# Five row buffers instead of four for the expert gathers of a one-core encoder block

## The chip, the cores and the metric

The kernel runs on one core of a Trainium2 chip. The metric is the device time of one execution in microseconds; the median of the runs shown counts.

## The reference, cut to what matters

One layer of a streaming encoder on 1024 tokens of width 1024: eight heads of stick-breaking attention and four mLSTM heads share an input projection, their outputs go through an output projection, and a PEER mixer follows. For this change only the mixer matters. Each token picks 128 of 16384 experts (8 heads, 16 each); expert e is one row of `expert_u` and one row of `expert_v`, 1024 floats each:

```
u   = take(expert_u, idx)            # 128 rows per token
act = gelu(einsum('td,tkd->tk', x, u))
vv  = take(expert_v, idx)
y   = einsum('tk,tkd->td', gate * act, vv)
```

## The kernel before, in words

The first part (to about 1400 us in the trace) is attention, mLSTM, output projection and routing. After that the mixer is computed for the 1024 tokens in two different ways that run beside one another.

**Gathered tokens.** The first 384 tokens (three tiles of 128, `NH` = 3) are done by `gather` (line 897). For each tile and each of its 128 choices k, GpSimd (POOL) issues an indirect DMA that fetches one row of U for each of the 128 tokens into a row buffer `gu` of 128x1024 floats (line 918), and VectorE (DVE) multiplies it with the tokens and sums along the row (line 920). When all 128 are done, ScalarE makes the gelu. Then the same with V: an indirect DMA into a row buffer `gv` (line 929), and DVE adds the row times its gate to `gy` (line 931). `gu` and `gv` have one tag and so share one set of `GU` buffers, used in turn. Two times 128 gathers for three tiles are 768, each of 128 rows of 4 KB. At a tile's end the buffers also take `x1` and `g2` (lines 933 to 942), and the result is written.

**Dense tokens.** The other 640 tokens are done by `dense` (line 1032): for each of 128 blocks of 128 experts, the block of U is loaded (`uf`, line 1015), split into two parts for TensorE (`uh`, `ul`, line 121 on ScalarE and line 125 on DVE), and multiplied with the tokens (`da`, lines 129 to 131); 24 of the blocks (`AHEAD`) were multiplied earlier and their gelu outputs `dg` are read back from memory (line 1012). `dg` is multiplied with the gates `dw` on DVE (line 1051) and split into `dgh` and `dgl`. The block of V is loaded into a single buffer `vf` (line 1042), split into `vh` and `vl`, and the second product runs in groups of three blocks: a part stays in PSUM (`yr`), another is copied out by ScalarE (`dt`, line 1092) and added on DVE (`dy`, line 1093). After the last block, line 1065 adds `x1` for eight row groups (`dx`) and line 1067 writes them.

**What sets the order.** `build` weaves the two generators (line 1208). A scheduler then fixes, when the program is built, the order of the instructions on each engine by its own estimate of how long each takes; on the chip each engine runs its own list in that order and waits on semaphores. So a DVE instruction that waits for a gather holds up the dense instructions behind it on DVE. The weights and blocks of U and V are issued from SyncE (SP), the gathers from POOL.

```
for k in range(ns):
    vv = g.tile([P, D], F32, tag="gu", name=f"gv{T}_{k}", bufs=GU)
    nc.gpsimd.indirect_dma_start(out=vv, out_offset=None, in_=a["V"],
                                 in_offset=bass.IndirectOffsetOnAxis(ap=idx[:, k : k + 1], axis=0))
    nc.vector.scalar_tensor_tensor(out=y, in0=vv, scalar=A[:, k : k + 1], in1=y, op0=ALU.mult, op1=ALU.add)
    yield G_STEP
```

Of the kernel before, what the change touches and what calls it, by code (L numbers as in the profile page):

```python
# [49 lines left out]
NB = 128  # L50

GB = 3
GU = 4
DG = 3
N_A = (8, 16)

# [56 lines left out]
class Kernel:  # L113
# [783 lines left out]
    def gather(self, T):  # L897
# [18 lines left out]
        for k in range(ns):  # L916
            u = g.tile([P, D], F32, tag="gu", name=f"gu{T}_{k}", bufs=GU)
            nc.gpsimd.indirect_dma_start(out=u, out_offset=None, in_=a["U"],  # L918
# [8 lines left out]
# [6 lines that stand above are left out]
        x1 = g.tile([P, D], F32, tag="gu", name=f"gx1_{T}", bufs=GU)  # L933
        if half:
            nc.sync.dma_start(x1[0:n], y[n:P])
            nc.vector.tensor_add(y[0:n], y[0:n], x1[0:n])
            x1 = g.tile([P, D], F32, tag="gu", name=f"gx2_{T}", bufs=GU)
        nc.sync.dma_start(x1[0:n], self.x1t_d[0:n, T])
        g2 = g.tile([P, D], F32, tag="gu", name=f"g2_{T}", bufs=GU)
        nc.sync.dma_start(g2[0:n], self.g2_d.partition_broadcast(n))  # L940
# [336 lines left out]
```

## Time and profile before

| | |
|---|---|
| Time, median of 3 runs | 3395.37 us (3392.22 to 3406.84) |
| The profiled execution | 3403.98 us, span 3402.3 us |
| Busy share of the span | PE 91%, DVE 79%, ACT 49%, POOL 44% |
| Mean granted TensorE clock | 0.957 |
| Moved | 799.51 MB, mean 235 GB/s |

The profiled execution is one run, 8.6 us above the median; sums over the trace are made against its own 3403.98 us. PE is TensorE, PEld its weight loads, DVE VectorE, ACT ScalarE, POOL GpSimd, SP SyncE. A wait is put down to the work whose end came last before the waiting engine went on.

### The profile page before, as it was taken

How to read it: one execution, taken by the hardware profiler on the slowest of the kernel's cores; microseconds unless marked ns; L12 is line 12 of the kernel's file. 1: busy time of each engine (PE TensorE's matmuls, PEld its weight loads, DVE VectorE, ACT ScalarE, POOL GpSimd, SP SyncE). 2: the span in 40 equal slices, each digit the busy share in tenths (PEclk: the TensorE clock that was granted, in tenths of full speed). 3: DMA queues.
4: the chain of work that ended last, by engine and by line, in shares of the span. 5: the costliest groups of instructions: out<-in, count | busy, mean ns of one | idle time of the engine just before them, and what ended most of it. 6: DMA issues, size and time to landing. Idle time of an engine off the chain costs nothing.

```text
span 3402.3 us, 53484 instructions
## 1 busy us (share of the span) xinstructions
PE 3085.2 (91%) x18581; PEld 2802.9 (82%) x18581; DVE 2698.6 (79%) x5464; ACT 1673.5 (49%) x3646; POOL 1493.9 (44%) x1334
## 2 busy tenths in 40 slices
PE   6998998998888789999899999999999999999993
PEld 4666676666666789999899999999999999999993
DVE  6776764589989858886778888888888887888887
ACT  4765677855675887885233333333333333333321
POOL 3000004545767334233455455565555545555554
PEclk8999998899989899999999999999999999999997
DMA  5243325532333545699888999998989998999988
GB/s 183 77 132 130 115 78 179 162 94 82 104 114 101 175 155 180 219 340 317 283 279 309 312 312 304 318 332 299 330 301 319 313 314 291 334 325 315 306 290 276
DMA packets 388864, 799.51 MB, mean 235 GB/s; under 512 B 35033, under 2 KB 216793, under 8 KB 386033
## 3 DMA queue, kind: packets, MB, share of 16 engines
q1 hardware_dynamic: 268368, 387.03, 34.7%
q0 software_dynamic: 110624, 402.77, 33.9%
q10 hardware_dynamic: 9600, 6.29, 0.6%
q8 instruction: 146, 2.39, 0.3%
q14 instruction: 126, 1.02, 0.1%
HBM read 716.23 MB, written 79.73 MB: 234 GB/s over the span
## 4 chain that ended last, share of the span: by engine, by line
PE 24%; DMA 21%; DVE 20%; issue 18%; POOL 10%; ACT 5%; SPq 1%; POOLq 0%; DVEq 0%; ACTq 0%
DMA gv<-in_V_dram,idx 11%; POOL gu L918 7%; DMA gu<-in_U_dram,idx 3%; DMA vf<-in_V_dram 3%; DVE gy L931 3%; POOL gv L929 2%; DVE gu L920 2%; PE wps L998 1%; PE da L129 1%; PE da L131 1%; PE da L130 1%; PE z L494 1%; ACT wm L994 1%; PE ipc L129 1%; PE ipc L131 1%
## 5 line engine op out<-in xcount | busy, mean ns | idle before, releaser
L918 POOL DMA_INDIRECT gu<-in_U_dram,idx x384 | 505.7, 1317 | 527.3 <-DVE gu L920 471.1
L929 POOL DMA_INDIRECT gv<-in_V_dram,idx x384 | 501.7, 1307 | 442.6 <-DVE gy L931 372.5
L931 DVE SCALAR_TENSOR_TENSOR gy<-gv,gA,gy 128x1024 f32<-128x1024 f32 x384 | 492.0, 1281 | 93.4 <-DMA gv<-in_V_dram,idx 88.8
L920 DVE SCALAR_TENSOR_TENSOR gu<-gu,gh 128x1024 f32<-128x1024 f32 x384 | 466.0, 1223 | 122.4 <-DMA gu<-in_U_dram,idx 116.9
L1092 ACT COPY dt<-dy 128x384 f32<-128x384 f32 x336 | 158.9, 480 | 455.0 <-PE dy L131 313.7
L129 PE MATMUL dy<-dgh,vh 128*128 128x384 f32 x1024 | 348.9, 344 | 34.6 <-ACT dt L1092 34.4
L129 PE MATMUL da<-dah,uh 128*128 128x384 f32 x1024 | 349.1, 341 | 10.9 <-ACT dg L946 6.4
L130 PE MATMUL dy<-dgl,vh 128*128 128x384 f32 x1024 | 348.6, 341 | 0.0
L131 PE MATMUL da<-dah,ul 128*128 128x384 f32 x1024 | 346.8, 339 | 0.5 <-DVE ul L125 0.5
L131 PE MATMUL dy<-dgh,vl 128*128 128x384 f32 x1024 | 347.3, 340 | 0.0
L130 PE MATMUL da<-dal,uh 128*128 128x384 f32 x1024 | 346.8, 339 | 0.0
L129 PE MATMUL yr<-dgh,vh 128*128 128x256 f32 x1024 | 286.6, 288 | 33.4 <-ACT dgh L121 21.2
L130 PE MATMUL yr<-dgl,vh 128*128 128x256 f32 x1024 | 292.0, 288 | 11.4 <-DVE dgl L125 11.2
L131 PE MATMUL da<-h2h,ul 128*128 128x256 f32 x1024 | 290.8, 284 | 0.0
L129 PE MATMUL da<-h2h,uh 128*128 128x256 f32 x1024 | 290.7, 284 | 0.0
L130 PE MATMUL da<-h2l,uh 128*128 128x256 f32 x1024 | 290.5, 284 | 0.0
L131 PE MATMUL yr<-dgh,vl 128*128 128x256 f32 x1024 | 287.3, 286 | 0.7 <-DVE vl L125 0.4
L121 ACT CAST vh<-vf 128x1024 fp32r<-128x1024 f32 x128 | 134.2, 1049 | 285.4 <-DMA vf<-in_V_dram 280.2
L125 DVE TENSOR_TENSOR vl<-vf,vh 128x1024 fp32r<-128x1024 f32 x128 | 156.4, 1222 | 93.1 <-ACT vh L121 92.8
L129 PEld LDWEIGHTS dy<-dgh,vh 128*128 128x128 f32 x1024 | 196.2, 192 | 40.1 <-ACT dt L1092 39.6
L125 POOL TENSOR_TENSOR vlm<-kvrm,vhm 128x128 fp32r<-128x128 f32 x56 | 30.3, 542 | 452.1 <-ACT vhm L121 442.9
L129 PEld LDWEIGHTS yr<-dgh,vh 128*128 128x128 f32 x1024 | 196.3, 195 | 37.4 <-ACT dgh L121 23.7
(435 smaller groups left out, 8941.0 us busy)
## 6 DMA issues: line engine op xcount, KB each, us to landing
uf<-in_UT_dram SPq DMA_DIRECT2D x128, 512.0 KB
vf<-in_V_dram SPq DMA_DIRECT2D x128, 512.0 KB
w_d<-wst SPq DMA_DIRECT2D x19, 2048.0 KB
dw<-w_d SPq DMA_DIRECT2D x32, 1216.0 KB
wfwq<-in_w_q_dram SPq DMA_DIRECT2D x192, 128.0 KB
wada<-in_w_adaT_dram SPq DMA_DIRECT2D x64, 256.0 KB
wfwo<-in_w_out_dram SPq DMA_DIRECT2D x96, 128.0 KB
wada<-in_w_adaT_dram SPq DMA_DIRECT2D x16, 512.0 KB
```

The costliest lines, as they stand in the source:

```text
L121: nc.scalar.copy(hi, src)
L125: e.tensor_sub(lo, src, hi.bitcast(F32))
L129: mm(out, sh, mh, start=start, stop=False, skip_group_check=skip)
L130: mm(out, sh, ml, start=False, stop=False, skip_group_check=skip)
L131: mm(out, sl, mh, start=False, stop=stop, skip_group_check=skip)
L494: mm(z[e], k[kx][r], q[qx][r, ts], start=i == 0, stop=i == 2 * len(k) - 2)
L918: nc.gpsimd.indirect_dma_start(out=u, out_offset=None, in_=a["U"], in_offset=bass.IndirectOffsetOnAxis(ap=idx[:, k : k + 1], axis=0))
L920: nc.vector.scalar_tensor_tensor(out=u, in0=u, scalar=1.0, in1=h2, op0=ALU.mult, op1=ALU.mult, accum_out=A[:, k : k + 1])
L929: nc.gpsimd.indirect_dma_start(out=vv, out_offset=None, in_=a["V"], in_offset=bass.IndirectOffsetOnAxis(ap=idx[:, k : k + 1], axis=0))
L931: nc.vector.scalar_tensor_tensor(out=y, in0=vv, scalar=A[:, k : k + 1], in1=y, op0=ALU.mult, op1=ALU.add)
L994: nc.scalar.activation(m[:, t], o1[:, :, t], AF.Copy, scale=i2g[:, 1, col])
L1092: nc.scalar.copy(t, ps)
```

## The change

```
-GU = 4
+GU = 5
```

The number of row buffers that `gu`, `gv`, and the `x1` and `g2` tiles share goes from four to five. Each takes 4 KB in every partition; the pool `gp` grows by that much into memory that nothing else holds at the time. No instruction is added or taken away. POOL waits, before it issues a gather, for the DVE instruction that read the buffer's last content: with four buffers that is the gather four back, with five the one five back. The scheduler, which plans with this, puts the gathers' instructions in other places among the dense ones.

On POOL, at the first gathers (`gu_0` is the first; what a row waits for is in brackets), before:

```order
L918 DMA gu_3_17980<-in_U_dram,idx 128x1024
L918 DMA gu_4_17983<-in_U_dram,idx 128x1024 [waits DVE_49]
L918 DMA gu_5_17986<-in_U_dram,idx 128x1024 [waits DVE_49]
```

and with the change:

```order
L918 DMA gu_3_17980<-in_U_dram,idx 128x1024
L918 DMA gu_4_17983<-in_U_dram,idx 128x1024
L918 DMA gu_5_17986<-in_U_dram,idx 128x1024 [waits DVE_49]
```

The fifth gather no longer waits for DVE; the order on POOL is the same but for one `dw` load that comes four gathers later.

On DVE, around the last block's multiply by the gates (line 1051, block 127; `gv_k` is choice k of the last tile), before:

```order
L125 TENSOR_TENSOR vl_35193<-vf_35190,vh_35192 128x1024
L1093 TENSOR_TENSOR dy<-dy,dt_35101 128x384
L931 SCALAR_TENSOR_TENSOR gy_32439<-gv_103_34767,gA_29433,gy_32439 128x1024
L1051 TENSOR_TENSOR dg_35131<-dg_35131,dw_34753 128x640
L931 SCALAR_TENSOR_TENSOR gy_32439<-gv_104_34840,gA_29433,gy_32439 128x1024
L125 TENSOR_TENSOR dgl_35198<-dg_35131,dgh_35197 128x640
```

and with the change:

```order
L125 TENSOR_TENSOR vl_35193<-vf_35190,vh_35192 128x1024
L1093 TENSOR_TENSOR dy<-dy,dt_35101 128x384
L931 SCALAR_TENSOR_TENSOR gy_32439<-gv_113_35113,gA_29433,gy_32439 128x1024
L1051 TENSOR_TENSOR dg_35131<-dg_35131,dw_34753 128x640
L931 SCALAR_TENSOR_TENSOR gy_32439<-gv_114_35116,gA_29433,gy_32439 128x1024
L125 TENSOR_TENSOR dgl_35198<-dg_35131,dgh_35197 128x640
```

The dense instructions stand alike; ten gathers that stood behind this place now stand ahead of it. Of the 768 gather instructions on DVE, 55 stood ahead of block 0's line 1051 and 59 do now, 389 and 397 ahead of block 64's, 744 and 754 ahead of block 127's.

On DVE, behind the last addition of line 1093, before:

```order
L1093 TENSOR_TENSOR dy<-dy,dt_35335 128x384
L1065 SCALAR_TENSOR_TENSOR dx_3_35371<-yr_17823,mod,dx_3_35371 128x256
L1065 SCALAR_TENSOR_TENSOR dx_3_35371<-dy,mod,dx_3_35371 128x384
L931 SCALAR_TENSOR_TENSOR gy_32439<-gv_111_35107,gA_29433,gy_32439 128x1024
L1065 SCALAR_TENSOR_TENSOR dx_4_35376<-yr_17824,mod,dx_4_35376 128x256
```

and with the change:

```order
L1093 TENSOR_TENSOR dy<-dy,dt_35335 128x384
L1065 SCALAR_TENSOR_TENSOR dx_3_35371<-yr_17823,mod,dx_3_35371 128x256
L1065 SCALAR_TENSOR_TENSOR dx_3_35371<-dy,mod,dx_3_35371 128x384
L931 SCALAR_TENSOR_TENSOR gy_32439<-gv_121_35207,gA_29433,gy_32439 128x1024
L1065 SCALAR_TENSOR_TENSOR dx_4_35376<-yr_17824,mod,dx_4_35376 128x256
```

Seventeen gathers (111 to 127) followed the last addition, now seven (121 to 127) do; the last of them stands ahead of `dx_6`, where it stood behind `dx_7`.

## Rows read from the trace of the kernel before

**Rows 1.** Windows by stage: window, length, busy time of each engine, clock, DMA share, GB/s.
```profile
1411.00:1600.00 189.00, 184.52 (x1317) 182.25 (x1316) 143.52 (x250) 149.35 (x402) 62.88 (x57) 0.99 0.91 325
1600.00:1800.00 200.00, 171.37 (x1098) 168.04 (x1097) 140.53 (x214) 58.80 (x95) 87.44 (x66) 0.94 0.83 282
1800.00:3340.00 1540.00, 1478.92 (x9863) 1467.00 (x9863) 1308.15 (x1634) 488.93 (x805) 834.30 (x627) 0.99 0.91 312
3340.00:3403.00 63.00, 9.86 (x60) 8.89 (x58) 42.12 (x49) 3.84 (x8) 23.49 (x20) 0.62 0.79 271
```
**Rows 2.** The page's chain that ended last, shares of the span by line.
```profile
DMA gv<-in_V_dram,idx 11%; POOL gu L918 7%; DMA gu<-in_U_dram,idx 3%; DMA vf<-in_V_dram 3%; DVE gy L931 3%; POOL gv L929 2%; DVE gu L920 2%; PE wps L998 1%; PE da L129 1%; PE da L131 1%; PE da L130 1%; PE z L494 1%; ACT wm L994 1%; PE ipc L129 1%; PE ipc L131 1%
```
**Rows 3.** The page's costliest groups: busy, mean ns, idle before and its releaser.
```profile
L918 POOL DMA_INDIRECT gu<-in_U_dram,idx x384 | 505.7, 1317 | 527.3 <-DVE gu L920 471.1
L929 POOL DMA_INDIRECT gv<-in_V_dram,idx x384 | 501.7, 1307 | 442.6 <-DVE gy L931 372.5
L931 DVE SCALAR_TENSOR_TENSOR gy<-gv,gA,gy 128x1024 f32<-128x1024 f32 x384 | 492.0, 1281 | 93.4 <-DMA gv<-in_V_dram,idx 88.8
```
**Rows 4.** The gather instructions by tile: durations (min/median/max), first and last start.
```profile
L918 POOL DMA_INDIRECT gu<-in_U_dram,idx x384: 935/1281/1987, 1411.2 to 3077.2; - x192
L929 POOL DMA_INDIRECT gv<-in_V_dram,idx x384: 935/1277/3151, 1816.2 to 3387.9; - x192
```
**Rows 5.** Waits of DVE, 1600 to 3340 us: total, times, longest.
```profile
DVE gu L920 <- DMA gu<-in_U_dram,idx: 97.6, 93, 3.4
DVE vl L125 <- ACT vh L121: 87.0, 35, 9.1
DVE gy L931 <- DMA gv<-in_V_dram,idx: 78.7, 85, 3.7
```
**Rows 6.** Waits of PE, 1600 to 3340 us.
```profile
PE dy L129 <- ACT dt L1092: 33.6, 17, 7.1
PE yr L129 <- ACT dgh L121: 21.2, 12, 3.6
PE yr L129 <- ACT vh L121: 12.3, 4, 4.3
PE yr L130 <- DVE dgl L125: 11.2, 9, 2.7
```
**Rows 7.** Waits of ACT, 1600 to 3340 us.
```profile
ACT vh L121 <- DMA vf<-in_V_dram: 280.2, 76, 11.2
...
ACT dt L1092 <- DVE dy L1093: 119.7, 46, 4.9
```
**Rows 8.** Timeline of DVE at the end: start, duration, instruction, idle before.
```profile
3336.88 0.82 DVE L1051 TENSOR_TENSOR dg<-dg,dw 128x640 f32<-128x640 f32 x1
...
3352.97 0.55 DVE L1093 TENSOR_TENSOR dy<-dy,dt 128x384 f32<-128x384 f32 x1
3358.71 0.48 DVE L1065 SCALAR_TENSOR_TENSOR dx<-yr,mod,dx 128x256 f32<-128x256 f32 x1 [5.19 <-DMA dx<-x_d]
...
3376.01 0.61 DVE L1065 SCALAR_TENSOR_TENSOR dx<-dy,mod,dx 128x384 f32<-128x384 f32 x1
...
3397.37 1.23 DVE L942 TENSOR_TENSOR gy<-gy,gx 128x1024 f32<-128x1024 f32 x1
```
**Rows 9.** The chain near the end: two gathers' way, issue to landing.
```profile
3375.97 6.45 DMA gv<-in_V_dram,idx
...
3387.95 6.75 DMA gv<-in_V_dram,idx
```
**Rows 10.** DMA queues, 1600 to 3400 us: packets, MB, share of 16 engines.
```profile
q0 software_dynamic: 102672, 373.86, 59.5%
q1 hardware_dynamic: 119037, 178.30, 30.2%
```
**Rows 11.** Timeline of POOL at the first gathers.
```profile
1415.32 0.94 POOL L918 DMA_INDIRECT gu<-in_U_dram,idx  x1 [0.30 <-issue]
1427.39 0.94 POOL L918 DMA_INDIRECT gu<-in_U_dram,idx  x1 [11.14 <-DVE gu L920]
```

## The prediction

> **What bounds the kernel now.** I read first the windows by stage, then the chain, then who waits for whom, and last the timeline of the end. The change touches nothing before the first gather at 1411.2 us [rows 4], so only what follows counts. There the windows [rows 1] show two things that are nearly full at once. PE is busy for 1650 of the 1740 us between 1600 and 3340 us (171.37 and 1478.92 added), so 90 us are idle. The DMA engines are at 0.83 and 0.91 at 282 and 312 GB/s. DVE is busy for 1449 us. From 3340 us on PE has 9.86 us of work left, and the end belongs to the gathers.
>
> The chain [rows 2] tells which of the two ends last. The gathers' way (DMA `gv` 11% and `gu` 3%, POOL's issues 7% and 2%, DVE's uses 3% and 2%) is 28% of the span, some 950 us; the `vf` loads are 3%, some 102 us. The gathers run in a circle: POOL waits for DVE to free a buffer (471.1 and 372.5 us) [rows 3], the rows fly, DVE uses them. One gather follows another every 2.58 us (1976.7 us from first start to last, over 767 steps) [rows 4], so a round of four buffers takes 10.3 us.
>
> The circle costs the dense work through DVE's list. DVE stands 176.3 us for gathers in flight (97.6 and 78.7) and 87.0 us for `vh` [rows 5], and what is behind it stands too. PE's own waits [rows 6] are 78.3 us in four rows.
>
> **The change, part by part.** No instruction is added. A gather may be issued when the DVE use five back is over, not the one four back, so up to one step, 2.58 us, earlier. The scheduler also moves the gathers forward in DVE's list: by 4 at the first dense block, by 10 at the last one.
>
> *The start.* The first four gathers leave by 1415.32 us and the fifth waits 11.14 us for DVE [rows 11]; it can now leave about 10.7 us earlier, 0.30 us behind the fourth's end. Nothing at the end hangs on this alone. I count it with the ten gathers below.
>
> *The dense stretch.* The 178 waits for gathers are 0.99 us each on average, the longest 3.7 us [rows 5]. If a gather left 2.58 us sooner and flew as long, nearly all would vanish; if it flew longer for having one more beside it, some would stay. I take half. What that is worth is read from PE. The waits for `dgh` (21.2) and `dgl` (11.2) come from DVE's list. `dt` (33.6 us) comes late either because DVE's additions are (119.7 us) or because ACT stands in front of a `vf` load (280.2 us) [rows 7]; I put half of it, 16.8 us, down to DVE. That makes 49 us, of which the gathers cause 176.3 in 263.3 (the rest is `vh`), so 33 us, and half of this is **16 us** off. The bounds are nothing, if PE then waits for `vf` instead, and the full 49 us.
>
> *The ten gathers more.* They must now be done before the dense work ends. Their DVE time, 10 times 1.281 us [rows 3], falls into a DVE that is idle for 15% of 1800 to 3340 us. Their bytes, 10 times 0.524 MB, would take 16.8 us at 312 GB/s if the DMA engines had no room, and nothing if they had; at a share of 0.91 [rows 1] the engines have 9% of 1540 us, some 139 us, to spare. So between 0 and 17 us on; I take **5 us**, nearer to the free end.
>
> *The end.* From the end of the last `dy` addition (3352.97 plus 0.55) to the end of the span (3402.3) it is 48.8 us [rows 8]. Seventeen gathers stand there now; with the change seven, of which five fit in buffers at once. With the `dx` steps as late as before, the use of 121 is over 7.4 us and that of 122 10.2 us behind that addition (one gather step behind each `dx` row, as before: 5.2 us of waiting, 1.1 of `dx`, 1.28 of use); the last gather is issued then and lands 6.75 us later [rows 9], so the last use ends near 18.5 us. But `dx_7` then decides: before, it was done at 3376.62, 23.1 us behind the addition; the final addition (1.23 us) stands behind it now, and its write takes as long as before, 3.7 us (3402.3 less 3398.60), so 28 us; the write of `dx_7` itself, at a flight of about 6.5 us, ends near 30. From 48.8 to 30 makes **19 us** off. Bounds: 10 us if `dx` itself gets later, 24 if it gets earlier with less traffic. This term rests on the two lists, not on a bandwidth, and I trust it most.
>
> The sum against the profiled execution: 3404.0 - 16 + 5 - 19 = 3374 us. That execution stands 8.6 us above the median of the runs, so against the median it is **3365 us**.
>
> **A rule weighed.** A gather takes 6.45 and 6.75 us from issue to landing at the end [rows 9]. The Trainium skill, page "DMA: Bandwidth & Descriptors", section "Anatomy of one DMA — SWDGE (gpsimd) path", fits 2.0 us plus the bytes over 436 GB/s, which for 0.524 MB is an estimate of 3.2 us from that page. The trace is at twice that. By that page more than half of a flight here would be queueing behind other transfers, which a fifth buffer makes longer, not shorter, and the sum would lose its 16 us; it is the first rival.
>
> **Rivals.** *The DMA engines are the bound.* With the share at 0.91 and moments without work between transfers, five gathers in flight would each fly five quarters as long at the same rate. Then the waits stay, the ten gathers cost their full 16.8 us, and only the end gains: 3395 + 17 - 19 = 3393 us. For it: even with PE done, 3340 to 3403 us shows 0.79 at 271 GB/s [rows 1], little more room than before. Against it: 325 GB/s at the same share of 0.91 between 1411 and 1600 us shows that 312 is no ceiling. It has 0.25. The page named above stands beside this rival.
>
> *The `vf` loads become the bound, slower.* `vf` has one buffer, and its landing is on the chain for 102 us; ACT stands for it 280.2 us [rows 7]. If the gathers, which hold 59.5% of the engines' time against 30.2% for the loads of SP [rows 10], took bandwidth from it and each landing took a quarter longer, as one more gather beside four might, the chain would grow by 26 us. With the ten gathers at full price and the end's gain this is 3395 + 26 + 17 - 19 = 3419 us. It decides from a landing about 19% longer (102 times 0.19 is 19, which with 17 - 19 gives the 17 us that a slower verdict takes). For it: PE's wait for `vh`, 12.3 us, is there already. Against: four gathers are in flight most of the time now, and the loads live with them. It has 0.12. The same page, section "Queues, rings and completion order", says that an engine goes round its queues packet by packet; by that, a longer gather queue takes no larger turn while both have work, and no run shown here tests it.
>
> *The circle is the whole bound.* All 49 us of PE's waits on DVE go, and the ten gathers are hidden: 3395 - 49 - 19 = 3327 us. For it: the 28% of the chain. Against: PE is at 95% of 1600 to 3340 us, and `vf` is next in line. It has 0.13.
>
> *The change doesn't do what it says.* The list of POOL excludes it: the fifth gather waits for nothing where it waited for DVE.
>
> **How the numbers follow.** The forecast has 0.50. A difference of 0.5%, 17 us, is about what a measurement of this kernel can tell from no change: faster is below 3378 us, slower above 3412. Of the forecast's 0.50, 0.44 lie below 3378 and 0.06 above, where the dense term comes out near nothing. With the 0.13 of the whole bound faster has 0.57; same has 0.06 and the 0.25 of the DMA bound, 0.31; slower has 0.12. The range goes from 3327, the whole bound, which I round to 3325, to the sum of the bad ends short of the slower rival: no dense gain, 17 us for the ten gathers and 10 us at the end, 3395 + 17 - 10 = 3402, rounded to 3403.
>
> **What would show it.** Right: from the last `dy` addition to the end about 30 us instead of 48.8; that addition about 11 us earlier than 3353 (16 less 5); DVE's waits for gathers between the same stages near 90 instead of 176 us; the DMA share of the dense stretch up by one or two hundredths. The first rival is right if the waits stay near 176 us and the last addition comes at about 3370 us. The second is right if ACT's 280.2 us for `vf` and PE's waits for `vh` and `dt` grow by tens of us. I am wrong altogether if the last gather still ends behind `dx_7`, since the lists then do not set the end as I read them.

## The result, and the profile after

Five row buffers take 3308.74 us (median of 6 runs, 3291.38 to 3317.85) where four take 3396.86 us (6 runs, 3383.64 to 3406.84): a ratio of 0.9732, 95% interval 0.971 to 0.9754; between the medians it is 88 us. The forecast was 3365 us with a range down to 3325, so the direction was right and the size far too small. The profiled execution has a span of 3303.2 us against 3402.3.

The windows by stage of the kernel after (window, length, busy time by engine, clock, DMA share, GB/s) answer to [rows 1]; the stages after 1800 us end about 100 us earlier:

```profile
1411.00:1600.00 189.00, 186.02 (x1338) 183.78 (x1336) 145.69 (x254) 150.27 (x404) 71.73 (x61) 1.00 0.92 338
1600.00:1800.00 200.00, 178.77 (x1158) 177.17 (x1159) 161.96 (x244) 61.57 (x99) 109.80 (x78) 0.94 0.91 317
1800.00:3240.00 1440.00, 1421.38 (x9646) 1418.60 (x9645) 1273.35 (x1590) 484.31 (x790) 846.35 (x611) 0.99 0.93 327
3240.00:3304.00 64.00, 29.75 (x191) 28.78 (x190) 47.79 (x59) 8.72 (x18) 23.48 (x20) 0.75 0.78 269
```

PE is idle for 40 us from 1600 to 3240 us, where it was idle for 90 us up to 3340, and the DMA engines move 327 instead of 312 GB/s. The gain is spread over the whole stretch. One and the same window of both kernels shows it, 1600 to 3200 us, first before and then after:

```profile
1600.00:3200.00 1600.00, 1516.42 (x10070) 1502.32 (x10069) 1328.67 (x1724) 505.61 (x829) 846.53 (x634) 0.98 0.91 310
```

```profile
1600.00:3200.00 1600.00, 1560.14 (x10528) 1555.77 (x10529) 1398.74 (x1797) 532.62 (x866) 928.93 (x672) 0.99 0.93 326
```

PE runs 10528 matmuls in it instead of 10070, 4.5% more, and POOL issues 672 gathers instead of 634, 6% more. Dense work and gathers have become faster together.

The gathers of the kernel after, by group (busy, mean ns, idle before and its releaser) and by tile (first and last start), answer to [rows 3, 4]:

```profile
L918 POOL DMA_INDIRECT gu<-in_U_dram,idx x384 | 521.4, 1358 | 455.9 <-DVE gu L920 373.6
L929 POOL DMA_INDIRECT gv<-in_V_dram,idx x384 | 528.7, 1377 | 367.6 <-DVE gy L931 316.3
L931 DVE SCALAR_TENSOR_TENSOR gy<-gv,gA,gy 128x1024 f32<-128x1024 f32 x384 | 491.1, 1279 | 15.0 <-DMA gv<-in_V_dram,idx 12.5
```

```profile
L918 POOL DMA_INDIRECT gu<-in_U_dram,idx x384: 932/1312/1990, 1411.8 to 2987.4; - x192
L929 POOL DMA_INDIRECT gv<-in_V_dram,idx x384: 932/1282/3555, 1779.7 to 3284.9; - x192
```

One gather follows another every 2.44 us (1873.1 us over 767 steps) where it was 2.58. Both kernels issue the first gather at the same time (1411.2 and 1411.8 us) and the last one 103 us apart, so this is the gain as the gathers see it. A round of five takes 12.2 us and a round of four took 10.3.

The waits of DVE and then of PE in the kernel after, 1600 to 3240 us (total, times, longest), answer to [rows 5, 6]:

```profile
DVE vl L125 <- ACT vh L121: 77.1, 33, 8.9
...
DVE gu L920 <- DMA gu<-in_U_dram,idx: 30.3, 30, 2.9
...
DVE gy L931 <- DMA gv<-in_V_dram,idx: 10.7, 17, 2.0
```

```profile
PE dy L129 <- ACT dt L1092: 16.9, 7, 8.3
PE yr L129 <- ACT vh L121: 15.4, 4, 5.9
PE da L129 <- ACT uh L121: 6.1, 1, 6.1
PE yr L129 <- ACT dgh L121: 1.7, 1, 1.7
PE yr L130 <- DVE dgl L125: 0.6, 1, 0.6
```

DVE stands for gathers in flight for 41.0 us instead of 176.3. PE's waits for what comes from DVE's list, `dgh` and `dgl`, fall from 32.4 to 2.3 us; what is left is `dt`, `vh` and `uh`. ACT's wait for `vf`, the answer to [rows 7], falls too:

```profile
ACT vh L121 <- DMA vf<-in_V_dram: 147.0, 55, 12.0
```

It was 280.2 us. The one `vf` buffer comes free when DVE has made `vl` from it, so a DVE that stands less can free it earlier; that this is why the wait fell is not shown by itself.

The timeline of DVE at the end of the kernel after answers to [rows 8]:

```profile
3273.11 0.55 DVE L1093 TENSOR_TENSOR dy<-dy,dt 128x384 f32<-128x384 f32 x1
3279.59 0.48 DVE L1065 SCALAR_TENSOR_TENSOR dx<-yr,mod,dx 128x256 f32<-128x256 f32 x1 [5.93 <-DMA dx<-x_d]
...
3292.19 1.28 DVE L931 SCALAR_TENSOR_TENSOR gy<-gv,gA,gy 128x1024 f32<-128x1024 f32 x1 [1.43 <-DMA gv<-in_V_dram,idx]
...
3296.26 1.22 DVE L941 TENSOR_TENSOR gy<-gy,g 128x1024 f32<-128x1024 f32 x1 [1.87 <-DMA g<-g_d]
...
3297.80 0.61 DVE L1065 SCALAR_TENSOR_TENSOR dx<-dy,mod,dx 128x384 f32<-128x384 f32 x1
3298.33 1.22 DVE L942 TENSOR_TENSOR gy<-gy,gx 128x1024 f32<-128x1024 f32 x1
```

From the end of the last `dy` addition (3273.66) to the end of the span it is 29.5 us, against 48.8. So the span's 99 us are 80 us from the dense stretch (3353.52 to 3273.66) and 19 us from the end.

### The profile page after: what moved, and what is told of

Read it like the earlier page. It is cut to its first block, busy times and chain, and to the rows that moved or that the text cites. A ratio compares the mean times of both kernels' runs of the same rounds, so it can differ in the third digit from the quotient of the medians.

```text
span 3303.2 us, 53461 instructions
## 1 busy us (share of the span) xinstructions
PE 3060.2 (93%) x18581; PEld 2790.1 (84%) x18581; DVE 2696.0 (82%) x5464; ACT 1678.0 (51%) x3646; POOL 1534.7 (46%) x1334
## 3 DMA queue, kind: packets, MB, share of 16 engines
q14 instruction: 125, 1.02, 0.1%
## 4 chain that ended last, share of the span: by engine, by line
PE 28%; issue 11%; DVE 11%; DMA 11%; POOL 8%; ACT 4%; SPq 0%; POOLq 0%; DVEq 0%; ACTq 0%
POOL gv L929 4%; PE da L129 4%; PE da L131 4%; PE da L130 4%; DMA vf<-in_V_dram 3%; POOL gu L918 3%; DMA gu<-in_U_dram,idx 2%; PE dy L129 2%; PE dy L130 2%; PE dy L131 2%; PE wps L998 2%; DVE gy L931 2%; PE yr L129 1%; PE yr L130 1%; PE yr L131 1%
## 5 line engine op out<-in xcount | busy, mean ns | idle before, releaser
L918 POOL DMA_INDIRECT gu<-in_U_dram,idx x384 | 521.4, 1358 | 455.9 <-DVE gu L920 373.6
L929 POOL DMA_INDIRECT gv<-in_V_dram,idx x384 | 528.7, 1377 | 367.6 <-DVE gy L931 316.3
L1093 DVE TENSOR_TENSOR dy<-dy,dt 128x384 f32<-128x384 f32 x336 | 184.6, 553 | 52.1 <-ACT dt L1092 48.4
L125 POOL TENSOR_TENSOR wlwq<-wfwq,whwq 128x256 fp32r<-128x256 f32 x192 | 149.6, 796 | 135.7 <-ACT whwq L121 130.5
```

Source lines behind the costliest of these rows:

```text
L125: e.tensor_sub(lo, src, hi.bitcast(F32))
L1093: nc.vector.tensor_add(y[:, i], y[:, i], t)
```

## The experiments

Theory A says that the buffer itself does it: DVE no longer stands for gathers in flight, and what is behind it in its list runs on. The rivals were the scheduler's new lists, the single `vf` buffer and the DMA engines' rate. Each run below is timed against the kernel before on its own chip; ratios are to that. The kernel before takes 3396.86 to 3400.77 us on these chips, so where medians of different chips are set beside one another some 4 us are uncertain. A trace is one execution, and executions of one kernel differ by 3 to 30 us.

**The gathers held back to their old places.** Five buffers, and the index of the first tile is made to depend on 33 small GpSimd operations (their result is zero):

```
+            nc.gpsimd.tensor_sub(z, h2[:, 0:NSEL], h2[:, 0:NSEL])
+            for _ in range(32):
+                nc.gpsimd.tensor_mul(z, z, h2[:, 0:NSEL])
+            nc.vector.tensor_copy(late, z)
+            nc.vector.tensor_tensor(out=late, in0=late, in1=idx, op=ALU.add)
+            idx = late
```

> Five buffers, but the first gather held back by a chain of 33 small GpSimd operations (about 0.55 us each) behind the load of gh2, so that the gathers stand on DVE where they stood with four buffers (49 ahead of the first dense block, 388 ahead of block 64, 744 ahead of block 127, 17 behind the last dy addition). Theory A (the buffer itself: DVE no longer stands for gathers in flight, so the dense work runs on; the places in the list only set the end): the last dy addition stays near 3274 us of the span, DVE's waits for gathers between 1600 and 3240 us stay near 41 us, and only the end comes back, 15 to 19 us, so about 3325 us. Rival B (the list does it: gathers that stand ten places earlier): the dense gain goes too and the time is back near 3390 us.

Measured: 3334.8 us, ratio 0.9804 (0.9749 to 0.9859), 26 us above five buffers. Its additions of `dy` on DVE, and DVE's waits for gathers between 1600 and 3240 us (`late` is the first tile's index; the lines are nine later in this kernel):

```profile
L1102 DVE TENSOR_TENSOR dy<-dy,dt x336: 497/552/589, 1684.0 to 3282.5; 128x384 f32<-128x384 f32 x168
```

```profile
DVE gu L929 <- DMA gu<-in_U_dram,idx: 25.8, 30, 3.7
...
DVE gu L929 <- DMA gu<-in_U_dram,late: 15.4, 13, 3.0
DVE gy L940 <- DMA gv<-in_V_dram,idx: 12.6, 19, 1.8
...
DVE gy L940 <- DMA gv<-in_V_dram,late: 7.7, 13, 1.7
```

The gathers are at their old places on DVE: 388 stand ahead of block 64, 744 ahead of block 127 and 17 behind the last addition. The waits stay low (61.5 us) and the last addition ends at 3283.0, 70 us earlier than with four buffers. The end takes 46 us again. So some 70 of the 80 us of the dense stretch are the buffer's at the old places, as theory A has it, and rival B falls. The places make most of the 19 us at the end. In the dense stretch the addition comes 9 us later than with five buffers alone, which is less than executions of one kernel differ by.

**The same 4 KB for `vf`.** Four row buffers:

```
-            vf = self.wr.tile([P, D], F32, tag="vf", name=f"vf{b}", bufs=1)
+            vf = self.wr.tile([P, D], F32, tag="vf", name=f"vf{b}", bufs=2)
```

> Four row buffers, and the same 4 KB given to a second vf buffer instead. Theory A (the circle of the gathers holds up DVE's list): DVE's waits for gathers stay near 176 us or grow, ACT's wait for vf (280 us) falls to below 100 us, PE gets back the 12 us of vh and part of dt, and the gain is 10 to 35 us (3360 to 3385 us). Rival C (the dense work is held by its single vf buffer, which DVE's late vl frees late): the gain is like that of the fifth row buffer, 70 us or more.

Measured: 3393.87 us, ratio 0.9993 (0.9971 to 1.0015): nothing, less than either theory gave. DVE's waits for gathers grew to 220.1 us between 1600 and 3305 us, as theory A had it, but ACT's wait for `vf` fell only to 237.1, not below 100. Its trace has the reason in three rows, the additions of `dy`, the gathers of V and PE's largest wait, 1600 to 3305 us:

```profile
L1093 DVE TENSOR_TENSOR dy<-dy,dt x336: 495/552/620, 1650.5 to 3337.9; 128x384 f32<-128x384 f32 x168
```

```profile
L929 POOL DMA_INDIRECT gv<-in_V_dram,idx x384: 932/1274/4025, 1795.0 to 3383.2; - x192
```

```profile
PE yr L129 <- ACT dgh L121: 50.2, 16, 5.9
```

The dense work ends 15 us earlier, but the gathers do not (last start 3383.2 against 3387.9), and they end the kernel. PE has only changed its wait: 50.2 us for `dgh`, which ACT makes from DVE's product of `dg` and the gates (line 1051). With four row buffers the gathers' circle holds both ends.

**Three row buffers.** `GU = 3`.

> Three row buffers. Theory A: a round of three must still hold one flight (about 6.5 us), one use (1.3 us) and one issue (about 2 us with its gap), 9.8 us, so a step takes at least 3.2 us where it took 2.58; 768 steps then end near 1411 + 2460 = 3870 us if the flight stays, near 3550 us if it shortens to 5.5 us and less; slower by 120 to 450 us. Rival D (the DMA engines are the bound, buffers matter little): slower by less than 30 us.

Measured: 3622.57 us, ratio 1.0652 (1.0603 to 1.0701), 223 us slower. The row buffers matter as theory A says, and the DMA engines are not the bound. The step is 2.88 us (1412.2 to 3617.6 over 767), under the 3.2 expected. A gather's flight is shorter with fewer under way: from issue to landing the median is 6.1 us for U and 5.4 for V here, and 7.8 and 7.5 in the run with six buffers below.

**The gathers nearly alone.** Four and five buffers, and 8 of the 128 dense blocks (the two tests for the last block are changed with it):

```
-        for b in range(NB):
+        for b in range(8):
```

> Four row buffers, and only 8 of the 128 dense blocks are done (the dense output is left incomplete), so that the gathers run alone for most of their time. Theory A (the circle: flight, use, issue, with queueing behind dense loads and DVE's list in it): alone, the flight is near 4.5 us, use 1.28, issue with its gap 1.9, so a round of about 7.7 us and a step of 1.9 us against 2.58 in the full kernel. Rival D (the DMA engines' rate for gathers): 0.524 MB at 340 GB/s, 1.54 us a step with either number of buffers.

> The same with five row buffers. Theory A: a step of 7.7/5, 1.54 us, about four fifths of that with four buffers, unless the DMA rate or GpSimd's issue (1.3 to 1.6 us) stops it just there. Rival D: the same step as with four.

Measured: 3039.22 and 2844.58 us, one run each. A window in which the gathers are alone, with four buffers and then with five:

```profile
2000.00:2400.00 400.00, 0.00 (x0) 0.00 (x0) 261.21 (x338) 0.31 (x1) 251.56 (x206) 0.50 0.81 274
```

```profile
2000.00:2400.00 400.00, 0.00 (x0) 0.00 (x0) 300.64 (x349) 0.31 (x1) 297.50 (x237) 0.50 0.90 315
```

206 gathers in 400 us are a step of 1.94 us (1.9 expected), 237 a step of 1.69 us (1.54 expected). The circle bounds them with four buffers, at 0.81 of the DMA engines. Its round is 7.8 us, as expected, but not from the parts expected: the median from issue to landing is 5.8 us for U and 5.5 for V, not 4.5. With five buffers the step shrinks by 13%, not by a fifth. Both limits that were named are then near, the DMA engines at a share of 0.90 and POOL busy for 297.5 of the 400 us; which of them holds was not tried.

**The dense work nearly alone.** Four buffers, two of the 128 choices gathered, in both loops:

```
-        for k in range(ns):
+        for k in range(2):
```

> Four row buffers, 2 instead of 128 choices gathered per half and tile (the gathered tokens' output is left incomplete), so that the dense work runs without the gathers. It shows what DVE's list and the shared DMA engines hold up in the full kernel. Theory A: the last dy addition comes within 60 us below that of five buffers (3274 us), 3215 to 3260 us, PE being nearly full there. Rival (PE itself is slowed by more than the gathers' waits, so the dense stretch was never near PE's own time): below 3200 us.

Measured: 3222.58 us (one run). The windows 1800 to 3200 us and 1600 to 3210 us, and the additions of `dy`:

```profile
1800.00:3200.00 1400.00, 1400.00 (x9552) 1400.00 (x9551) 561.56 (x704) 478.24 (x777) 0.00 (x0) 1.00 0.34 103
1600.00:3210.00 1610.00, 1607.82 (x10956) 1607.50 (x10954) 648.61 (x820) 549.86 (x896) 0.00 (x0) 1.00 0.34 104
```

```profile
L1094 DVE TENSOR_TENSOR dy<-dy,dt x336: 547/557/560, 1637.4 to 3209.4; 128x384 f32<-128x384 f32 x168
```

PE is never idle between 1800 and 3200 us and the last addition ends at 3210. That misses theory A's range (3215 to 3260) by 5 us and is above the 3200 of its rival. The gathers, with all that they take of DVE and the DMA engines, thus held the dense work up by 143.5 us with four buffers (3353.5), and by 64 us with five.

**Less traffic.** Five buffers, and the dense blocks use one kept block of U:

```
-        uf = ua.tile([P, KB, P], F32, tag="uf", name=f"uf{b}", bufs=2)
-        nc.sync.dma_start(uf, a["UT"][b])
+        if self.dn_open:
+            uf = self.uf_kept
+        else:
+            uf = self.uf_kept = ua.tile([P, KB, P], F32, tag="uf", name=f"uf{b}", bufs=2)
+            nc.sync.dma_start(uf, a["UT"][b])
```

> Five buffers, and the dense blocks multiply one kept block of U, so that 104 loads of 0.5 MB are left out (the output of the dense tokens is then another one). Theory A with PE as the bound after the change: these loads are a ninth of the traffic of the stretch, but PE is idle for only some 44 us from 1600 us on, so 15 to 40 us faster than five buffers, not below 3265 us. Rival D (the DMA engines bound the five-buffer kernel): 54 MB at 327 GB/s are 166 us; 100 us or more faster.

Measured: 3369.72 us, ratio 0.991 (0.988 to 0.9939): 61 us slower than five buffers, with 104 loads fewer. Both expectations miss. The scheduler wrote other lists: 608 gathers stand ahead of block 96 on DVE instead of 573, all 768 ahead of the last `dy` addition, and ACT waits 347.7 us for `vf`. The run shows that bytes alone do not set this time (1800 to 3240 us moves 292 GB/s at a share of 0.85); it doesn't measure what the U loads cost, since the lists moved with them.

**Six row buffers, with two `dg` buffers to make room, and its control.** `GU = 6` and `DG = 2`; the control is `GU = 5` and `DG = 2`.

> Six row buffers; to make room, two dg buffers instead of three. If the fifth buffer has taken nearly all that DVE stood for (41 us of waits for gathers are left), the sixth brings 5 to 20 us over five row buffers with two dg buffers, 3285 to 3305 us; no gather stands behind the last dy addition and the dx rows set the end. Rival E (each buffer is worth the same, the circle still bounds): another 70 us, 3240 us.

> Five row buffers and two dg buffers: the control for the runs that make room in this way. Within 10 us of five row buffers alone, 3300 to 3318 us, with the end up to 10 us later where the dx rows go round in two buffers.

Measured: 3346.08 us with six (ratio 0.9843, 0.9799 to 0.9887) and 3323.53 with five (0.9771, 0.9727 to 0.9816). The control is 15 us above five buffers alone, just outside what was expected, but the two ratios' intervals overlap, so what the third `dg` buffer is worth is not clear of noise. The sixth row buffer loses 22.5 us against the control, on the same chip. Six buffers' largest waits of PE, 1600 to 3240 us, and their gathers:

```profile
PE yr L129 <- ACT vh L121: 68.6, 17, 9.2
PE yr L129 <- ACT dgh L121: 15.6, 1, 15.6
```

```profile
L929 POOL DMA_INDIRECT gv<-in_V_dram,idx x384: 932/1275/2951, 1753.2 to 3258.0; - x192
```

The gathers run on (last start 3258.0, against 3296.4 in the control), the last `dy` addition comes at 3333.4, and PE waits for `vh`. Two explanations were open: the lists put the gathers too far ahead, or the single `vf` buffer had become PE's wait.

**Six row buffers, started later.** The chain of GpSimd operations again, 71 of them, with `GU = 6` and `DG = 2`. The gates' tile `gA` also goes round in one buffer here instead of two; no wait for it shows among DVE's.

> Six row buffers, two dg buffers, and the first gather held back by a chain of 71 small GpSimd operations (some 38 us, behind gh2's load), so that 46 instead of 62 gathers stand ahead of the first dense block. Theory F (what six buffers lost, 23 us against five with two dg buffers, they lost because the list puts the gathers too far ahead of the dense work: the gathers are done 75 us before the last dy addition, and PE works alone at the end): a later start gives back some of it, 3315 to 3335 us, with the last dy addition 10 to 30 us earlier. Rival (six buffers crowd the DMA engines and so slow the vf loads at any start): no faster than 3346 us.

Measured: 3378.21 us, ratio 0.9936 (0.9913 to 0.9959). Slower still by 32 us, and PE waits 95.7 us for `vh` between 1600 and 3240 us. The start did move the list back (582 gathers stand ahead of block 96 on DVE, 602 in the run before), but the last `dy` addition ends later (3381.7 against 3333.9), not earlier. Theory F, that a later start gives time back, falls.

**Six row buffers with a second `vf` buffer, and its control.** The second `vf` buffer costs no memory: every second block of V goes into the memory of the index tiles `i1` and `i2`, which nothing reads once the gate matrices are built (the two are allocated as one tile `i12`). With `GU = 6`, `DG = 2`; the control has `GU = 5`, `DG = 3`:

```
-            vf = self.wr.tile([P, D], F32, tag="vf", name=f"vf{b}", bufs=1)
+            if b % 2:
+                vf = self.i12.rearrange("p x a b c -> p (x a b c)")[:, 0:D]
+            else:
+                vf = self.wr.tile([P, D], F32, tag="vf", name=f"vf{b}", bufs=1)
```

> Six row buffers, two dg buffers and the same second vf buffer. Theory H (six row buffers lost 23 us because vf, in one buffer, became the wait of PE: 68.6 us for vh): with the second vf buffer PE's waits for vh fall below 15 us and the time falls below that of five row buffers with two vf buffers, 3245 to 3270 us. Rival F (the lists put the gathers too far ahead of the dense work, whatever vf does): PE still waits, for dgh or dgl, and the time stays above 3300 us.

> Five row buffers, three dg buffers, and every second block of V loaded into the memory of the two index tiles, which is free by then: a second vf buffer that costs no memory. Sixteen gathers stand behind the last dy addition on DVE. Theory G (with the second vf buffer PE is full until about 3225 us, and the gathers end last, at the circle's pace of some 2.4 us a step): 3265 to 3285 us, PE idle for less than 15 us between 1600 and 3200 us. Rival (dg's third buffer matters still): 3250 to 3262 us.

Measured: 3255.83 us with six (ratio 0.9586, 0.9559 to 0.9614), the fastest of all runs, and 3274.16 us with five (0.9645, 0.962 to 0.9671). PE's two largest waits with six, 1600 to 3200 us, and the window 1800 to 3200 us:

```profile
PE yr L129 <- ACT dgh L121: 16.3, 1, 16.3
PE yr L130 <- DVE dgl L125: 1.8, 2, 1.2
```

```profile
1800.00:3200.00 1400.00, 1398.85 (x9536) 1398.25 (x9535) 1271.82 (x1583) 473.85 (x777) 891.30 (x614) 1.00 0.95 335
```

The waits for `vh` are gone, and the sixth buffer, which lost 22.5 us with one `vf` buffer, gains 18 us with two, although it had to give up a `dg` buffer. That is what theory H gave, for the waits and for the time. This pair alone does not exclude rival F, because the list moved too: 578 gathers stand ahead of block 96 where 602 stood with one `vf` buffer. But the run with the later start has nearly this list (399 ahead of block 64 and 582 ahead of block 96, 398 and 578 here) with one `vf` buffer, and it waits for `vh` and is 122 us slower. That speaks for the single `vf` buffer as the cause of the loss, and against the places. In the control PE is as full, and there the gathers end the kernel, as theory G had it (last start 3256.3, last `dy` addition 3229.6). With six buffers the last start is 3220.4, and the last use of a gather and the last addition end together (3236.5 and 3237.9).

**Five row buffers, two `vf` buffers, with two and with four `dg` buffers.** The first is `GU = 5`, `DG = 2` and `bufs=2` for `vf`; the second also takes `i1` and `i2` in turn as `dg` buffers.

> Five row buffers and two vf buffers; to make room, two dg buffers instead of three. Theory A with vf next in line: of the 40 us that PE still waits between 1600 and 3240 us, 16.9 (dt) and 15.4 (vh) hang on vf, so 10 to 30 us faster than five row buffers alone, 3280 to 3300 us, if two dg buffers cost nothing. Rival: the end is then set by the gathers (seven behind the last dy addition, each step 2.4 us) or by the dx rows, which go round in two dg buffers, and it is not faster than 3308 us.

> Five row buffers and two vf buffers, with dg going round in four: two of its own pool and, once the gate matrices are built, the two index tiles i1 and i2, which are as large and no longer needed. Two dg buffers instead of three cost 15 us with five row buffers (3323.5 against 3308.7), and two vf buffers brought 48 us over that (3275.3). If the two terms add, 10 to 20 us faster than the run with both and two dg buffers: 3255 to 3268 us. If TensorE is already the bound there (it was idle for some 40 us after 1600 us), no faster than 3270 us.

Measured: 3275.31 us (ratio 0.9639, 0.9596 to 0.9681) and 3277.11 us (0.9649, 0.9622 to 0.9676). The second `vf` buffer is worth 48 us with five row buffers and two `dg` buffers, where it was worth nothing with four (and three `dg` buffers); against five row buffers alone the first run is 33 us faster, just over the 10 to 30 us expected. The extra `dg` buffers bring nothing beside it, so the expected sum of the two terms is a miss: PE is already full (1399.80 of the 1400 us from 1800 us on in the second) and the gathers end last.

## Why the prediction was wrong

*What bounds the kernel:* right about the chain. The gathers' circle was what ended last, and the buffer relieved it. Wrong about how the circle reaches PE, as below.

*The start:* right. The fifth gather left 0.30 us behind the end of the fourth, at 1417.09 us instead of 1427.39. (The rows of the prediction give 10.8 us for this, not 10.7.)

*The end:* right, 19 us forecast and 19.3 measured; the last use of a gather stands ahead of `dx_7`, as the list had it. That the size is so close is luck in part: `dx_7` was done 24.8 us behind the last addition, not 23.1, as DVE stood 1.87 us for the load of `g` ahead of it, and the end came 4.8 us behind `dx_7`, not the 6.5 taken for its write.

*The ten gathers more:* forecast as 5 us on. No cost of theirs shows: with the gathers held back the dense stretch ends 9 us later, not earlier, within what executions differ by.

*The dense stretch:* this step failed. It priced the relief at 16 us, with 49 us as the upper bound, and 80 us came (11 forecast with the ten gathers). Two things in it were too small. First, "I take half" of DVE's waits: three quarters went, 176.3 to 41.0 us. Second, and more, "What that is worth is read from PE": I took PE's named waits for the most that could be won, and put down only some of them to DVE. The windows from 1600 us to the end of the last addition, before and then after:

```profile
1600.00:3353.52 1753.52, 1660.14 (x11018) 1643.93 (x11016) 1462.09 (x1866) 551.57 (x907) 928.88 (x700) 0.98 0.90 309
1600.00:3273.66 1673.66, 1629.90 (x10992) 1624.55 (x10992) 1467.23 (x1872) 554.60 (x905) 976.94 (x707) 0.99 0.93 325
```

PE's idle time fell by 50 us (93.4 to 43.8), and its busy time by 30 us. So the busy time, which the prediction left as it was, was no floor; in the run without gathers PE is busy for 1607.8 us from 1600 us on (10956 matmuls). Of the 30 us some 4 are work that was done before 1600 us (26 fewer matmuls here, at 0.15 us). Up to 13 are the clock: in these two stretches the granted clock stood at the lower of its two levels, 1.2 instead of 2.4 GHz, for 68 us before and 42 us after. That time goes with PE's idle time in the same stretch of the other runs: 188 us where PE was idle for 199 (three buffers), 8 where it was idle for 14 (five buffers and the spare `vf`), none where it was idle for 2 (without gathers). The rest of the 30 us was not taken apart.

A third part may be the round over `vf`: ACT's wait for it halved, which I had counted only as a rival's loss. No run shows its share.

The size could have been read another way, from the step. DVE's list ties 5.4 gathers to every dense block (689 over 127 blocks before, 695 after), so a stretch whose end the circle sets is as long as its steps: 768 times the 0.135 us by which the step shrank is 104 us. This is the gain told again and no forecast, because the new step could not be known from the trace of four buffers alone. A round of five took 12.2 us; at 10.3 us, as with four, the step would have shrunk most, and at 12.9 us, five old steps, nothing would have been won.

*The rivals.* That the DMA engines are the bound is refuted for four buffers: 327 GB/s and 41 us of waits instead of 312 and 176, and three buffers cost 223 us. That `vf` becomes the bound did not happen at five, and did at six, with the sign that was given for it: PE waits for `vh`. The circle as the whole bound came nearest, in its mechanism and with its 3327 us; its price of 49 us for the dense stretch had the same cap in it. By the rule weighed beside the first rival, the Trainium skill's page "DMA: Bandwidth & Descriptors", section "Anatomy of one DMA — SWDGE (gpsimd) path", more than half of a flight would be queueing. Whether it is, no run shows: with four buffers and 8 dense blocks the median flight is still 5.8 and 5.5 us, where the estimate from that page is 3.2, and gathers fly beside one another there too. It doesn't follow from queueing that one more buffer brings nothing, for the flights did get longer with more buffers (6.1 and 5.4 us with three, 7.8 and 7.5 with six) and the step still shrank.

Not settled: how the 80 us divide between DVE holding PE directly and through `vf`. Each way shows in a run, the first with two `vf` buffers and four row buffers (50.2 us for `dgh`), and a wait for `vh` that a second `vf` buffer ends with six; that the second way had a share with four is not shown.

## What to carry to other kernels

Where one engine's list serves two streams, a buffer that is short in one stream holds up the other as well, and the gain can be larger than the waits that the other stream's engine shows (here 80 us against 49). It is the change of the circle's step times its steps, which here was known only from the trace afterwards. Busy time is then no floor either. After such a relief look which single buffer the other stream has: the second `vf` buffer was worth nothing before the fifth row buffer and 48 us behind it, and the sixth row buffer turned from a loss into a gain with it.

## What the runs showed of the hardware that was not expected

How long GpSimd takes to issue a gather differs from run to run, though the instruction is the same. The median is 1.28 us in the full kernel with four buffers and 1.01 to 1.02 with three; in the runs with 8 dense blocks it is 0.94 to 0.96 us with four and 0.99 to 1.02 with five. What makes it longer was not tried.

The DMA engines at a share of 0.97 moved 354 GB/s between 1411 and 1600 us (six row buffers with two `vf` buffers), so the 312 GB/s of the kernel before was no ceiling of theirs.
